# Weight tiles of the T-form matmuls placed by 64-byte residue: high parts at 64, low parts at 0 modulo 128

## The chip, the cores and the metric

The kernel runs on one core of one Trainium2 chip. The metric is the device time of one execution in microseconds; the number quoted is the median over runs. One further execution was profiled; its rows are what the prediction reads.

## What is computed

The reference is a block of two layers followed by a second block, for 256 tokens of width 1024, all in float32:

```python
for l in range(2):
    h = _rmsnorm(x, norm_mix[l])
    p_rw, p_sb, p_ret, p_conv = jnp.split(h @ w_in[l], MIX_SPLITS, axis=-1)
    branches = (_rwkv7_mixer(p_rw, ...), _stick_breaking_mixer(p_sb, ...),
                _retention_mixer(p_ret, ...), _conformer_conv_mixer(p_conv, ...))
    merged = sum(sigmoid(h @ w_gate[l, i]) * (branches[i] @ w_branch[l, i]) for i in range(4))
    x = x + merged @ w_out[l]
    h = _rmsnorm(x, norm_ffn[l])
    x = x + (_swiglu(h, ffn_w1, ffn_w3, ffn_w2) if l == 0 else _moe_ffn(h, router, moe_w1, moe_w3, moe_w2))
x = second_block(x, ...)     # attention and a recurrence on h @ w_in_2, then w_out_2
```

(The sum over branches is written shorter here than in the source.) What matters for this change is that nearly all of the time goes into products of activations with weight matrices that are read once from HBM. The feed-forward of layer 0 is 1024 by 2816; that of layer 1 is a mixture of eight experts.

## The kernel before, in words

**Split products.** A float32 product is made of three float32r matmuls. A weight block of 128 by 1024 floats (4096 bytes per partition) arrives in a `raw` tile; `wsplit_` (L258) makes a high part `wh` on ScalarE (L271) and a low part `wl = raw - wh` on VectorE (L272). The activations have been split the same way, into `hh` and `hl` (in other stages `uh`/`ul`, `bh`/`bl`, `mh`/`ml`, and so on). Each product is then `wh` with the high activations, `wh` with the low ones, and `wl` with the high ones, summed in one PSUM bank. All matmuls go through one wrapper and carry line L131 in the profile.

**Two forms.** In the T form the weights are the stationary operand, 128 by 128, and 256 tokens of an activation tile are streamed past them, so that every matmul has a weight load of its own:

```python
if kind == "T":
    ps = ((h[:, kk, off:off + n], ah), (h[:, kk, off:off + n], al), (o[:, kk, off:off + n], ah))
```

(`dense`, L332; `h` is `wh`, `o` is `wl`, `ah` and `al` are the activations; the feed-forward's second product, `down` at L1792, does the same.) In the other form the activations are stationary and up to 512 columns of the weights are streamed. The program has 5,904 T-form matmuls of 256 columns. The layers' input projections, gates, branch outputs, the feed-forward of layer 0, and most of the second block are T form; the experts and a few input columns are the other form.

**Slots.** `slot` (L242) hands out the tiles in turn. Pool `wp` has three slots for `raw` and three for each of `wh` and `wl`; a stage can add spare slots of its own pool with `spare` (L254). The feed-forward of layer 0 has two split slots of its own (`spare(fp, 4, 2)`, L1785): its split blocks go to three `wp` slots, then two of its own, and round again, 24 matmuls to each block. The mixture of experts has two of its own as well.

**Addresses.** The tiles lie in SBUF in the order in which they are first asked for. `pad` (L168) takes up bytes between them. The activations of the layers were padded to a start of 0 modulo 128 bytes. In the built program, starts modulo 128 bytes are:

| tile | before | with the change |
|---|---|---|
| `wp` slots, `wh` / `wl` | 64 / 64 | 64 / 0 |
| feed-forward's own slots, `wh` / `wl` | 0 / 0 | 64 / 0 |
| experts' own slots, `wh` / `wl` | 64 / 64 | 64 / 64 |
| `hh`, `hl`, `uh`, `ul`, `mh`, `ml`, `nr` | 0 | 0 |
| `bh`, `bl` of the branches, but for one | 0 | 0 |
| `bl` of branch 0 in layer 0 | 64 | 64 |
| `yah` in the second block | 96 | 96 |
| experts' activations `xg`, `mu` | 64 | 64 |

Columns inside a weight tile are taken in steps of 128 floats (512 bytes), rows of a tile in steps of 1024 or more bytes, so every operand has the residue of its tile.

The order of the work is set by a scheduler that takes priorities from the code (`tc.high_priority`) and a few dependencies written out by hand.

Of the kernel before, what the change touches and what calls it, by code (L numbers as in the profile page):

```python
# [18 lines left out]
P = 128  # L19
# [89 lines left out]
def build(tc, I, out, dbg=None, upto=99):  # L109
# [11 lines left out]
    wp = es.enter_context(tc.tile_pool(name="wp", bufs=4))  # L121
# [26 lines left out]
    def bank(tag="mx"):  # L148
        return pp.tile([P, 512], F32, name=tag, tag=tag, bufs=4)
# [18 lines left out]
    def pad(pool, n, nm):  # L168

        pool.tile([P, n // 4], F32, name=nm, tag=nm, bufs=1)  # L170
# [55 lines left out]
    def wsplit(raw, k, n, perm=False):  # L226

        with tc.high_priority(offset=HP[0]):
            return wsplit_(raw, k, n, perm)

    HP = [0, 0]


    more = {"pool": None, "raw": 0, "split": 0, "few": 0, "lead": 0}
    turn = {"raw": 0, "split": 0}


# [1 line left out]
    lead = {"n": 0, "ops": (), "hold": (), "late": None}  # L239
    behind = []  # L240

    def slot(kind, shapes):  # L242
        own = more[kind]
        n = 3 + own
        t_ = n - 1 if more["few"] else turn[kind] % n
        turn[kind] += 1
        at = min(more["lead"], own)

        if t_ < at or t_ >= at + 3:
            t_ -= 3 * (t_ >= at)  # L250
            return [more["pool"].tile(sh, dt, name=nm, tag=f"{nm}x{t_}", bufs=1) for nm, sh, dt in shapes]
        return [wp.tile(sh, dt, name=nm, tag=nm, bufs=3) for nm, sh, dt in shapes]

    def spare(pool, raw, split_, lead=0):  # L254
        more.update(pool=pool, raw=raw, split=split_, few=0, lead=lead)
        turn.update(raw=0, split=0)

    def wsplit_(raw, k, n, perm):  # L258
        h, o = slot("split", [("wh", [P, 1024], F32R), ("wl", [P, 1024], F32R)])
        h = h[:, :k * n].rearrange("p (k n) -> p k n", n=n)  # L260
        o = o[:, :k * n].rearrange("p (k n) -> p k n", n=n)
        if perm:
            for g in range(2):
                src = raw[:, :, g * 256:(g + 1) * 256].rearrange("p k (b d) -> p k b d", d=64)
                hv = h.rearrange("p k (b g d) -> p k g b d", g=2, d=64)[:, :, g]
                ov = o.rearrange("p k (b g d) -> p k g b d", g=2, d=64)[:, :, g]
                for kk in range(k):
                    S.copy(out=hv[:, kk], in_=src[:, kk])
                    V.tensor_sub(out=ov[:, kk], in0=src[:, kk], in1=hv[:, kk])
        else:  # L270
            a = S.copy(out=h, in_=raw)  # L271
            i = V.tensor_sub(out=o, in0=raw, in1=h)  # L272
            if lead["n"]:
                lead["n"] -= 1
                if lead["late"] and not lead["n"]:
                    tc.add_manual_dep(i.ins, lead["late"].ins.name, nosync, reason="choice first")
                for x, y in zip((a, i), lead["ops"]):
                    tc.add_manual_dep(x.ins, y.ins.name, nosync, reason="activations first")
                for r in lead["hold"]:
                    tc.add_manual_dep(r.ins, i.ins.name, nosync, reason="first half first")  # L280
                lead["hold"] = ()
            if behind:
                for x, y in zip((a, i), behind.pop(0)):
                    tc.add_manual_dep(x.ins, y.ins.name, nosync, reason="norm first")
        return h, o

    def wload(src, k, n, rows=False, pinned=False, halves=False):
        with tc.high_priority(offset=HP[1]):
            return wload_(src, k, n, rows, pinned, halves)
# [222 lines left out]
    def run(g):  # L512
        for _ in g:
            pass
# [10 lines left out]
    def mix_layer(l):  # L525
        with ExitStack() as ls_:
# [315 lines left out]
            def raised():  # L842
                HP[0], HP[1] = 500, 500
                yield
# [202 lines left out]
            for g in range(2):  # L1047
                _, gb = dense(I["w_gate"][l, 0], g * 512, 512, KC, hact, TJ)
                if g:
                    HP[0], HP[1] = 0, 0  # L1050
                for c in range(2):
# [329 lines left out]
    def second():  # L1381
        W = I["w_in_2"]
        with ExitStack() as ss_:
# [26 lines left out]
            next(lg)  # L1410
            HP[0], HP[1] = 500, 500
            run(lg)
# [362 lines left out]
    for l in range(2):  # L1775
        if upto < 2 * l + 1:
            break
        mix_layer(l)

        if upto < 2 * l + 2:  # L1780
            break
        if l == 0:
            with ExitStack() as fs:
                fp = fs.enter_context(tc.tile_pool(name="ffn", bufs=2, reuse_waits="tile"))
                spare(fp, 4, 2)  # L1785
                placed(None)
                hact = norm(gains("nf", l, 2), fp, "fth", 12, halves=True)
                accs = [bank() for _ in range(4)]
                first = {}
                F = 2816  # L1790

                def down(f0, uh, ul):  # L1792

                    for k0, ks, h, o in wstream(I["ffn_w2"][0][f0 * P:(f0 + 2) * P], 0, 1024, 2):
                        for kk in range(ks):
                            kc = f0 + k0 + kk
                            a0, a1 = uh[:, k0 + kk], ul[:, k0 + kk]
                            for b in range(KC):
                                acc = accs[b // 2][:, (b % 2) * T:(b % 2 + 1) * T]
                                cs = slice(b * P, (b + 1) * P)  # L1800
                                for q, (x_, m_) in enumerate(((h[:, kk, cs], a0), (h[:, kk, cs], a1), (o[:, kk, cs], a0))):
                                    st = kc == 0 and q == 0
                                    i = TE.matmul(acc, x_, m_, start=st and b % 2 == 0, stop=kc == F // P - 1 and q == 2, skip_group_check=True)
                                    if st and b % 2 == 0:
                                        first[b // 2] = i
                                    elif st:
                                        tc.add_manual_dep(i.ins, first[b // 2].ins.name, nosync, reason="bank order")

                ready = []
                for g0 in range(0, F, 512):  # L1810
                    cn = min(512, F - g0)
                    jobs = [("T", 128 * c, 128) for c in range(cn // P)]
                    _, ba = dense(I["ffn_w1"][0], g0, cn, KC, hact if g0 else late["early"], jobs)
                    if g0 == 0:
                        late["finish"]()
                    tts = []
                    for c in range(cn // T):
                        th = fp.tile([P, 512], F32, name="fth", tag="fth", bufs=12)
                        a_ = ba[2 * c]
                        if g0 == 0:  # L1820
                            a_ = fp.tile([P, 512], F32, name="fsc", tag="fth", bufs=12)
                            V.tensor_tensor(out=a_.rearrange("p (a b) -> p a b", b=T), in0=ba[2 * c].rearrange("p (a b) -> p a b", b=T), in1=late["rsb"], op=OP.mult)
                        S.activation(out=th, in_=a_, func=AF.Tanh, scale=0.5)
                        V.scalar_tensor_tensor(th, th, 1.0, a_, op0=OP.add, op1=OP.mult)
                        tts.append(th)
                    for r in ready:
                        down(*r)
                    ready = []
                    _, bb = dense(I["ffn_w3"][0], g0, cn, KC, hact, jobs)
                    for c in range(cn // T):  # L1830
                        th = tts[c]
                        V.tensor_tensor(out=th, in0=th, in1=bb[2 * c], op=OP.mult)
                        uh = fp.tile([P, 2, T], F32R, name="uh", tag="uh", bufs=4)
                        ul = fp.tile([P, 2, T], F32R, name="ul", tag="ul", bufs=4)
                        split(th.rearrange("p (a b) -> p a b", b=T), uh, ul)
                        ready.append((g0 // P + 2 * c, uh, ul))
                    if g0 == LL[0]:
                        lc = late_constants(fp, late_loads(fp))
                    if g0 >= LL[1]:
                        next(lc, None)  # L1840
                placed("ffn")
                run(lc)
                for r in ready:
                    down(*r)
                for q in range(4):
                    residual(accs[q], 2 * q)
                spare(None, 0, 0)
        else:
            moe(gains("nf", l, 2))
        dump(f"xf{l}", xT)  # L1850
# [37 lines left out]
```

## Time and profile before

| | |
|---|---|
| median of 3 runs | 1419.56 us (1419.38 to 1420.79) |
| profiled execution | 1418.68 us, its span 1416.9 us |
| TensorE (PE) busy | 1361.9 us, 96% of the span, 10,953 matmuls |
| weight loads (PEld) | 1262.1 us, 89%, 10,953 loads |
| VectorE (DVE) busy | 1078.2 us, 76% |
| ScalarE (ACT) busy | 805.4 us, 57% |
| mean granted TensorE clock | 0.992 |
| HBM | 292 MB moved, 206 GB/s over the span |

How to read it: the busy time of a matmul in the trace is the time from its start to the end of its last write, and neighbours overlap; a matmul that is reported with 282 ns can follow its predecessor after 113 ns. The time that a stretch of matmuls takes is therefore read from the starts in the timeline: last start minus first start, divided by the number of steps between them. Busy shares count overlapping work once.

### The profile page before, as it was taken

How to read it: one execution, taken by the hardware profiler on the slowest of the kernel's cores; microseconds unless marked ns; L12 is line 12 of the kernel's file. 1: busy time of each engine (PE TensorE's matmuls, PEld its weight loads, DVE VectorE, ACT ScalarE, POOL GpSimd, SP SyncE). 2: the span in 40 equal slices, each digit the busy share in tenths (PEclk: the TensorE clock that was granted, in tenths of full speed). 3: DMA queues.
4: the chain of work that ended last, by engine and by line, in shares of the span. 5: the costliest groups of instructions: out<-in, count | busy, mean ns of one | idle time of the engine just before them, and what ended most of it. 6: DMA issues, size and time to landing. Idle time of an engine off the chain costs nothing. (4 is left out here: it accounts for less than half of the span.)

```text
span 1416.9 us, 26493 instructions
## 1 busy us (share of the span) xinstructions
PE 1361.9 (96%) x10953; PEld 1262.1 (89%) x10953; DVE 1078.2 (76%) x1569; ACT 805.4 (57%) x1126; POOL 51.3 (4%) x65
## 2 busy tenths in 40 slices
PE   6999989999999899999998899999999999999998
PEld 6989979999999889988898788888888887998997
DVE  5669867685655585897576798998998999676765
ACT  5543264564444454324544688788788777465653
POOL 0000010001000100002000000000000002010000
PEclk9999999999999999999999899999999999999999
DMA  7553125586565345412457799899899896743352
GB/s 257 182 170 104 62 94 194 190 301 207 180 139 204 119 141 179 148 62 96 131 186 278 246 363 368 280 375 360 293 379 339 309 339 209 228 145 120 103 135 91
DMA packets 138098, 294.24 MB, mean 208 GB/s; under 512 B 6981, under 2 KB 29517, under 8 KB 137712
## 3 DMA queue, kind: packets, MB, share of 16 engines
q1 hardware_dynamic: 134720, 283.14, 58.0%
q0 software_dynamic: 3168, 9.31, 2.7%
q8 instruction: 87, 1.43, 0.4%
q14 instruction: 43, 0.35, 0.1%
q10 hardware_dynamic: 80, 0.02, 0.0%
HBM read 289.82 MB, written 2.62 MB: 206 GB/s over the span
## 5 line engine op out<-in xcount | busy, mean ns | idle before, releaser
L272 DVE TENSOR_TENSOR wl<-raw,wh 128x1024 fp32r<-128x1024 f32 (+1 forms) x542 | 633.5, 1187 | 220.8 <-ACT wh L271 215.1
L271 ACT CAST wh<-raw 128x1024 fp32r<-128x1024 f32 (+1 forms) x542 | 549.2, 1022 | 424.4 <-PE mm L131 336.0
L131 PE MATMUL mm<-hh,wl 128*128 128x256 f32 x1376 | 388.0, 282 | 5.6 <-DVE wl L272 3.1
L131 PE MATMUL mm<-hh,wh 128*128 128x256 f32 x1376 | 391.1, 284 | 2.3 <-ACT hh L223 1.6
L131 PE MATMUL mm<-hl,wh 128*128 128x256 f32 x1376 | 389.9, 283 | 0.2 <-DVE hl L224 0.2
L131 PEld LDWEIGHTS mm<-hh,wl 128*128 128x128 f32 x1376 | 260.7, 190 | 7.5 <-DVE wl L272 3.5
L131 PEld LDWEIGHTS mm<-hh,wh 128*128 128x128 f32 x1376 | 261.0, 190 | 6.7 <-issue 2.7
L131 PEld LDWEIGHTS mm<-hl,wh 128*128 128x128 f32 x1376 | 260.8, 190 | 3.4 <-issue 1.8
L131 PE MATMUL mm<-wh,xg 128*128 128x512 f32 (+1 forms) x768 | 229.4, 374 | 0.0
L131 PEld LDWEIGHTS mm<-wh,xg 128*128 128x128 f32 x768 | 142.6, 188 | 20.0
L131 PE MATMUL mm<-wl,xg 128*128 128x512 f32 (+1 forms) x384 | 142.6, 371 | 0.0
L131 PE MATMUL mx<-wh,mu 128*128 128x512 f32 x352 | 117.3, 394 | 0.0
L131 PEld LDWEIGHTS mm<-wl,xg 128*128 128x128 f32 x384 | 72.2, 188 | 9.9
L131 PEld LDWEIGHTS mx<-wh,mu 128*128 128x128 f32 x352 | 66.1, 188 | 12.7
L131 PE MATMUL mx<-wl,mu 128*128 128x512 f32 x176 | 68.8, 391 | 0.0
L975 DVE SCALAR_TENSOR_TENSOR cac<-cu,pcd,cac 128x256 f32<-128x256 f32 x120 | 52.8, 477 | 0.1
L131 PE MATMUL mx<-uh,wh 128*128 128x256 f32 x176 | 49.0, 281 | 1.4 <-ACT uh L223 1.4
L131 PE MATMUL mx<-ul,wh 128*128 128x256 f32 x176 | 49.4, 281 | 0.0
L131 PE MATMUL mx<-uh,wl 128*128 128x256 f32 x176 | 49.2, 280 | 0.0
L131 PE MATMUL mm<-nr,wh 128*128 128x256 f32 x192 | 36.8, 287 | 3.7 <-ACT nr L460 2.1
L131 PEld LDWEIGHTS mx<-wl,mu 128*128 128x128 f32 x176 | 33.1, 188 | 5.6
L131 PE MATMUL mm<-bh,wh 128*128 128x256 f32 x128 | 35.6, 281 | 0.2 <-DVE gth L1031 0.2
(686 smaller groups left out, 2065.2 us busy)
## 6 DMA issues: line engine op xcount, KB each, us to landing
raw<-in_moe_w_dram SPq DMA_DIRECT2D x104, 1024.0 KB
raw<-in_w_in_dram SPq DMA_DIRECT2D x42, 1024.0 KB
raw<-in_ffn_w_dram SPq DMA_DIRECT2D x33, 1024.0 KB
raw<-in_w_gate_dram SPq DMA_DIRECT2D x32, 1024.0 KB
raw<-in_moe_w_dram SPq DMA_DIRECT2D x32, 768.0 KB
raw<-in_w_out_dram SPq DMA_DIRECT2D x12, 1024.0 KB
raw<-in_w_branch_dram SPq DMA_DIRECT2D x8, 1024.0 KB
raw<-in_moe_w_dram SPq DMA_DIRECT2D x8, 512.0 KB
```

Of the source, the lines that this page charges most:

```text
L131: i = getattr(nc.tensor, name)(*a, **k)
L271: a = S.copy(out=h, in_=raw)
L272: i = V.tensor_sub(out=o, in0=raw, in1=h)
L975: V.scalar_tensor_tensor(acc[:, b], cu[:, b, 2 + k:2 + k + T], dw[:, 2 * k + b:2 * k + b + 1], acc[:, b], op0=OP.mult, op1=OP.add)
```

## The change

The change moves tiles and nothing else. A new helper `tile_` allocates the split tiles: in `wp` it puts a pad of 64 bytes ahead of the first `wl` tile and one of 448 behind the last; in a stage that asks for it (`shift=1`, the feed-forward of layer 0) it pads 64 bytes ahead of the first own `wh` tile, makes the own `wh` and `wl` tiles 1040 floats wide, of which the same 1024 are used, and pads 192 bytes behind the last. The pads add up so that all other tiles move by 512 or 1024 bytes and keep their residues modulo 512. The instructions of every engine and queue, and their order, are the same as before; only addresses differ.

```diff
--- before.py
+++ after.py
@@ -228,10 +228,12 @@
         with tc.high_priority(offset=HP[0]):
             return wsplit_(raw, k, n, perm)
 
+
+    SHIFT = (64, 448), (0, 0), (64, 192)
     HP = [0, 0]
 
 
-    more = {"pool": None, "raw": 0, "split": 0, "few": 0, "lead": 0}
+    more = {"pool": None, "raw": 0, "split": 0, "few": 0, "lead": 0, "shift": 0}
     turn = {"raw": 0, "split": 0}
 
 
@@ -248,11 +250,26 @@
 
         if t_ < at or t_ >= at + 3:
             t_ -= 3 * (t_ >= at)
-            return [more["pool"].tile(sh, dt, name=nm, tag=f"{nm}x{t_}", bufs=1) for nm, sh, dt in shapes]
-        return [wp.tile(sh, dt, name=nm, tag=nm, bufs=3) for nm, sh, dt in shapes]
-
-    def spare(pool, raw, split_, lead=0):
-        more.update(pool=pool, raw=raw, split=split_, few=0, lead=lead)
+            return [tile_(more["pool"], sh, dt, nm, f"{nm}x{t_}", 1) for nm, sh, dt in shapes]
+        return [tile_(wp, sh, dt, nm, nm, 3) for nm, sh, dt in shapes]
+
+    seen = set()
+
+    def tile_(pool, sh, dt, nm, tag, bufs):
+
+        new, own = (id(pool), tag) not in seen, pool is not wp
+        seen.add((id(pool), tag))
+        lo, hi = SHIFT[1 + more["shift"] if own else 0]
+        if new and tag == ("whx0" if own else "wl") and lo:
+            pad(pool, lo, "padw")
+        wide = {(False, "wl"): 1024}.get((own, nm), 1040 if own and more["shift"] else sh[1])
+        t = pool.tile([P, wide], dt, name=nm, tag=tag, bufs=bufs) if nm != "raw" else pool.tile(sh, dt, name=nm, tag=tag, bufs=bufs)
+        if new and tag == (f"wlx{more['split'] - 1}" if own else "wl") and hi:
+            pad(pool, hi, "padz")
+        return t
+
+    def spare(pool, raw, split_, lead=0, shift=0):
+        more.update(pool=pool, raw=raw, split=split_, few=0, lead=lead, shift=shift)
         turn.update(raw=0, split=0)
 
     def wsplit_(raw, k, n, perm):
@@ -1782,7 +1799,7 @@
         if l == 0:
             with ExitStack() as fs:
                 fp = fs.enter_context(tc.tile_pool(name="ffn", bufs=2, reuse_waits="tile"))
-                spare(fp, 4, 2)
+                spare(fp, 4, 2, shift=1)
                 placed(None)
                 hact = norm(gains("nf", l, 2), fp, "fth", 12, halves=True)
                 accs = [bank() for _ in range(4)]
```

## Rows read from the trace of the kernel before

**Rows 1.** Page: busy time and chain of waits (chain shares of the span by engine).

```profile
PE 1361.9 (96%) x10953; PEld 1262.1 (89%) x10953; DVE 1078.2 (76%) x1569; ACT 805.4 (57%) x1126; POOL 51.3 (4%) x65
PE 41%; DVE 2%; ACT 1%; issue 0%; POOL 0%; DVEq 0%; ACTq 0%
```

**Rows 2.** Windows: stretch (us), its length, PE busy (instructions), clock, DMA share, GB/s.

```profile
225.00:300.00 75.00, 74.79 (x639) 1.00 0.66 222
300.00:480.00 180.00, 176.45 (x1481) 1.00 0.59 182
...
785.00:1190.00 405.00, 404.88 (x2045) 0.99 0.92 329
```

**Rows 3.** Groups of matmuls by form: busy us, mean ns; 128x256 is the T form.

```profile
L131 PE MATMUL mm<-hh,wh 128*128 128x256 f32 x1376 | 391.1, 284 | 2.3 <-ACT hh L223 1.6 <-DVE pcv L213 0.4 <-ACT wh L271 0.3
...
L131 PE MATMUL mm<-wl,xg 128*128 128x512 f32 x256 | 99.8, 390 | 0.0
L131 PE MATMUL mx<-wl,mu 128*128 128x512 f32 x176 | 68.8, 391 | 0.0
```

**Rows 4.** Timeline, PE: start us, duration us; first and last start, feed-forward, `wp` slots.

```profile
325.08 0.28 PE L131 MATMUL mm<-hl,wh 128*128 128x256 f32 x1
...
330.52 0.28 PE L131 MATMUL mx<-ul,wh 128*128 128x256 f32 x1
```

**Rows 5.** Timeline, PE, feed-forward, the own slots that follow.

```profile
330.87 0.28 PE L131 MATMUL mx<-ul,wh 128*128 128x256 f32 x1
...
336.27 0.28 PE L131 MATMUL mx<-ul,wh 128*128 128x256 f32 x1
```

**Rows 6.** Timeline, PE, feed-forward later: `wp` slots, first and last start.

```profile
350.66 0.28 PE L131 MATMUL mm<-hl,wh 128*128 128x256 f32 x1
...
358.79 0.28 PE L131 MATMUL mm<-hl,wh 128*128 128x256 f32 x1
```

**Rows 7.** Timeline, PE, feed-forward later: own slots.

```profile
359.02 0.28 PE L131 MATMUL mm<-hh,wh 128*128 128x256 f32 x1
...
364.42 0.28 PE L131 MATMUL mx<-uh,wh 128*128 128x256 f32 x1
```

**Rows 8.** Timeline, PE, layer 0: branch outputs 3, 1 and 2, first and last.

```profile
223.29 0.28 PE L131 MATMUL mm<-bh,wh 128*128 128x256 f32 x1
...
238.93 0.28 PE L131 MATMUL mm<-bh,wh 128*128 128x256 f32 x1
```

**Rows 9.** Timeline, PE, layer 0: branch output 0, two stretches without a pause.

```profile
240.92 0.28 PE L131 MATMUL mm<-bh,wl 128*128 128x256 f32 x1
...
242.10 0.28 PE L131 MATMUL mm<-bh,wl 128*128 128x256 f32 x1
...
242.68 0.28 PE L131 MATMUL mm<-bh,wl 128*128 128x256 f32 x1
...
245.16 0.28 PE L131 MATMUL mm<-bh,wl 128*128 128x256 f32 x1
```

**Rows 10.** Timeline, PE, layer 0: the last gate, first and last start.

```profile
245.28 0.28 PE L131 MATMUL mm<-hh,wh 128*128 128x256 f32 x1
...
267.53 0.28 PE L131 MATMUL mm<-hh,wh 128*128 128x256 f32 x1
```

**Rows 11.** Timeline, PE: 512 weight columns past `hh`/`hl`, then past `xg` in the experts.

```profile
72.59 0.39 PE L131 MATMUL mm<-wh,hh 128*128 128x512 f32 x1
...
83.55 0.39 PE L131 MATMUL mm<-wh,hl 128*128 128x512 f32 x1
...
799.93 0.39 PE L131 MATMUL mm<-wl,xg 128*128 128x512 f32 x1
...
802.65 0.39 PE L131 MATMUL mm<-wl,xg 128*128 128x512 f32 x1
```

**Rows 12.** Instructions on tile `wl`, VectorE, 301 to 476 us: ns min/median/max.

```profile
L272 DVE TENSOR_TENSOR wl<-raw,wh x62: 1217/1225/1227, 300.4 to 475.1; 128x1024 fp32r<-128x1024 f32 x62
```

## The prediction, before the run

> **What bounds the kernel.** I read the page first. TensorE is busy for 96% of the span and its weight loads for 89%, so a load runs beside the matmul ahead of it; the chain of waits that ended last names hardly anything but PE [rows 1]. The chain stops early, so I checked it by stage with the windows view: in the gates and branch outputs of layer 0 PE is busy for 74.79 of 75.00 us, in the feed-forward for 176.45 of 180, in the experts for 404.88 of 405, with the clock granted in full or nearly [rows 2]. What changes the step from one matmul to the next therefore reaches the end of the kernel almost undiminished. The table of matmul forms says where the matmuls are: 1,376 each of the three products with `hh`/`hl`, and smaller groups, 5,904 in T form in all [rows 3]. Its mean of 284 ns is no price, since neighbours overlap. Prices come from the timeline, as last start minus first start over the steps between.
>
> **What an address costs, as the trace of before shows it.** The feed-forward holds the comparison ready-made: its blocks go to three `wp` slots (weights at 64, activations at 0 modulo 128; I call that *opposite*), then to two own slots (both at 0, *equal*). Stage, engines and clock are the same. Opposite: 325.08 to 330.52 is 48 steps in 5.44 us, 113.3 ns each [rows 4]. Equal: 330.87 to 336.27 is 45 steps in 5.40 us, 120.0 ns [rows 5]. So residues matter by 6.7 ns a matmul. But opposite is not always that fast: later in the same stage 69 steps take 8.13 us, 117.8 ns [rows 6], while the own slots still take 45 steps in 5.40 us, 120.0 ns [rows 7]. The fast pace also holds in branch outputs 3, 1 and 2, 138 steps in 15.64 us, 113.3 ns [rows 8]. It comes and goes with the same addresses, mostly after a pause or a change of operand. I call the two a *fast* and a *slow* pace of opposite operands. The stage of mostly T-form work gives the mean over both: 75.00 us over 639 matmuls, 117.4 ns [rows 2].
>
> **The change part by part.** No instruction is added, removed or moved on any engine or DMA queue; there is no new wait. Only the spacing of matmuls, and of the engines that read or write the moved tiles, can change.
>
> *VectorE and ScalarE* write the tiles at other residues. In the feed-forward the low parts of `wp` and own slots, at 64 and at 0, take 1217 to 1227 ns, median 1225 [rows 12]. I cost this at nothing, and by the spread of that row a difference of 10 ns on 542 splits could be 5 us of VectorE time at most, in stages where it has slack beside PE.
>
> *T-form matmuls.* A triple now has two loads at 64 and one at 0, all against activations at 0. By neighbouring pairs that is opposite, opposite, equal. Layer 0 holds one stage with such a triple: branch output 0, where it is the low activations that lie at 64 beside weights at 64, so that of three pairs one is equal. There 10 steps take 1.18 us and 21 steps 2.48 us, 3.66 us over 31, 118.1 ns [rows 9]. It follows directly on the fast stretch [rows 8] and does not keep its pace. The slow pace of the gate right behind it, 189 steps in 22.25 us, is 117.7 ns [rows 10]. I take 118.1 ns for every T-form matmul, since this is the only row with the new mixture, against a mean of 117.4: 5,904 x 0.7 ns = **+4.1 us**. In this mean the feed-forward's 26 own blocks gain (26 x 24 x 1.9 ns = 1.2 us), and the rest loses, above all where it was fast. The bounds: if the fast pace holds and only the equal pair pays, (2 x 113.3 + 120.0)/3 = 115.5 ns, 5,904 x -1.9 = -11 us; if the slow one does, (2 x 117.8 + 120.0)/3 = 118.5, +6.5 us. Outside those lie fast everywhere, 113.3, -24 us, and 120.0 everywhere, +15 us.
>
> *The experts* stream weights past `xg` and `mu`, all at 64 so far, 12 steps in 2.72 us, 226.7 ns for 512 columns. With residues apart, as past `hh`/`hl`, 47 steps take 10.96 us, 233.2 ns [rows 11]. Here it is equal that is cheaper. Of the 256 + 176 low products of that width [rows 3], three in five lie in `wp` slots and now stand apart: 259 x 6.5 = **+1.7 us**, at least nothing, and at most 2.2 us if 77 narrower ones pay too. The 64 low products of 512 columns past activations at 0 go the other way: **-0.4 us**.
>
> The sum is +4.1 + 1.7 - 0.4 = +5.4 us. On the profiled execution, 1418.68 us, that is 1424.1; the median of the runs shown stands 0.88 us above it, so the forecast for the median is **1424.9 us**. A measurement of this kernel tells about 0.2% (2.8 us) from no change.
>
> **A rule against the rows.** The rows 4 and 5 show weights read from two residues at 113.3 and 120.0 ns with all else alike. The Trainium skill, page "SBUF — State Buffer", section "SBUF: two separate sides", states that TensorE has ports of its own and never waits on another reader, and the section on bandwidth pools gives its weight loads a second, independent read port. By that rule no address would matter and the sum would be 0, 1419.6 us; the trace disagrees by 6.7 ns a matmul.
>
> **The rivals.**
>
> *Faster, the slow pace is broken.* If the slow pace is a lock between two streams of constant distance, a load that is displaced by 64 bytes once in three may keep it from forming, and the triple costs two fast steps and an equal one, 115.5 ns: 1419.6 - 11 + 1 = about 1410 us. The new rows would decide it by whether 117.8 is seen at all. For it: the fast pace exists with the very same addresses. Against it: the mixed stage left the fast pace at once [rows 8, 9], and the own slots, equal for 48 matmuls on end, did not break the slow one [rows 6, 7]. I give it 0.22, and 0.10 more to something faster still or to gains by halves (113.3 ns everywhere would be 1395 us).
>
> *No change that can be measured.* The gain of the own blocks (1.2 to 2.8 us, the latter if they come to 115.5), a part of the fast stretches kept, and experts that pay nothing, together cancel the loss; or residues act otherwise than by pairs, and paces are drawn anew with a mean near 117.4. That gives 1417 to 1422 us. 0.20, of which a few hundredths stand for residues that do not matter at all, as if what I read as their price were the own slots' place.
>
> *Worse than forecast.* The equal load drags the whole triple to 120.0 ns, as when all three are equal [rows 5, 7]: 5,904 x 2.6 = +15 us, 1435 us. 0.04.
>
> *The forecast*, triples near 118 ns: 0.44.
>
> **How the numbers follow.** The forecast and the worse case give slower 0.48; no change 0.20; faster 0.32. The range goes from the broken lock, 1409 us (1419.6 - 11, experts free), to the slow pace with its equal load and the experts at full price, 1419.6 + 6.5 + 2.2 = 1428.3 us. It leaves out the all-fast case and the 120 ns case. The forecast's own range is 1421.5 to 1428.3 us.
>
> **What would show it.** Right: in the profile of the changed kernel the steps in the gates and input projections stand near 118 ns, no long stretch at 113.3 is left, the feed-forward's own blocks come down from 120.0, and low products of the experts in `wp` slots step at over 230 ns. Wrong: long stretches at 115.5 or less, which would mean that the mixed stage of layer 0 misled me because there it was the streamed operand that jumped by 64 bytes and not the loaded one; or experts at 227 ns throughout, which takes 1.7 us off.

## The result, and the profile after

The changed kernel takes **1426.91 us** (median of 6 runs, 1424.53 to 1428.93) against 1419.62 us (6 runs) for the kernel before on the same chip: ratio 1.0052, 95% interval 1.0038 to 1.0065. It is slower by 7.3 us. The forecast was 1424.9 us, within a range to 1428.3.

The profiled execution of the changed kernel was the slowest of its six, 1428.93 us with a span of 1427.2 us; that of the kernel before was, with 1418.68 us, quicker than all of its runs. Part of the 10.3 us between the two spans is therefore the draw of two executions, and the text keeps that part apart.

The page of the changed kernel, busy times and chain:

```profile
PE 1372.8 (96%) x10953; PEld 1268.9 (89%) x10953; DVE 1079.0 (76%) x1569; ACT 805.0 (56%) x1126; POOL 51.4 (4%) x65
PE 40%; DVE 2%; ACT 1%; issue 1%; POOL 0%; ACTq 0%; DVEq 0%
```

Beside [rows 1], PE's busy time has grown by 10.9 us with the same 10,953 matmuls, and its weight loads by 6.8; VectorE and ScalarE stand within 1 us of where they were. The low tiles take as long to write as in [rows 12], here on VectorE from 305 to 482 us (min/median/max in ns):

```profile
L289 DVE TENSOR_TENSOR wl<-raw,wh x61: 1217/1225/1228, 305.3 to 479.3; 128x1024 fp32r<-128x1024 f32 x61
```

The same three stretches as in [rows 2], each moved by as much as the stage now starts later (length, then PE, weight loads, VectorE, ScalarE and GpSimd busy, then clock, DMA share, GB/s):

```profile
227.70:302.70 75.00, 75.00 (x638) 74.77 (x637) 59.13 (x77) 40.91 (x52) 0.52 (x1) 1.00 0.64 221
304.70:484.70 180.00, 176.44 (x1469) 174.66 (x1469) 106.29 (x137) 78.13 (x90) 8.21 (x15) 0.99 0.58 179
791.80:1196.80 405.00, 404.63 (x2030) 348.52 (x2031) 373.18 (x398) 317.20 (x372) 1.02 (x2) 1.00 0.92 329
```

PE has no new gap in these stages; it gets through fewer matmuls in the same time: 2,030 for 2,045 in the experts, 1,469 for 1,481 in the feed-forward. The two differ in kind. In the feed-forward the clock of 0.99 holds one stretch of 3.4 us at half the clock, which by itself costs some 14 steps (an estimate: half of 3.4 us over 118 ns); outside it the mean T-form step there is 117.9 ns against 118.0. In the experts the steps themselves are longer. The groups by form say which kinds (busy us, mean ns), first of the changed kernel:

```profile
L131 PE MATMUL mm<-hl,wh 128*128 128x256 f32 x1376 | 391.9, 285 | 0.2 <-DVE hl L224 0.2
L131 PE MATMUL mm<-hh,wh 128*128 128x256 f32 x1376 | 391.8, 285 | 2.3 <-ACT hh L223 1.6 <-DVE pcv L213 0.4 <-ACT wh L288 0.3
L131 PE MATMUL mm<-wh,xg 128*128 128x512 f32 x512 | 163.7, 394 | 0.0
L131 PE MATMUL mx<-wh,mu 128*128 128x512 f32 x352 | 118.2, 397 | 0.0
L131 PE MATMUL mm<-wl,xg 128*128 128x512 f32 x256 | 100.6, 393 | 0.0
L131 PE MATMUL mx<-wl,mu 128*128 128x512 f32 x176 | 69.2, 393 | 0.0
```

Then the experts' high products in the kernel before, which the prediction had not looked at:

```profile
L131 PE MATMUL mm<-wh,xg 128*128 128x512 f32 x512 | 162.2, 391 | 0.0
...
L131 PE MATMUL mx<-wh,mu 128*128 128x512 f32 x352 | 117.3, 394 | 0.0
```

The low products went up as forecast, from 99.8 to 100.6 and from 68.8 to 69.2 [rows 3]; but so did the high ones, by 1.5 and 0.9 us, although their tiles had not moved.

The timeline of the changed kernel, first and last start of the stretches that [rows 4], [rows 5], [rows 8] and [rows 11] hold (start us, duration us):

```profile
329.79 0.28 PE L131 MATMUL mm<-hl,wh 128*128 128x256 f32 x1
...
335.44 0.28 PE L131 MATMUL mx<-ul,wh 128*128 128x256 f32 x1
...
335.79 0.28 PE L131 MATMUL mx<-ul,wh 128*128 128x256 f32 x1
...
341.11 0.28 PE L131 MATMUL mx<-ul,wh 128*128 128x256 f32 x1
...
226.02 0.28 PE L131 MATMUL mm<-bh,wh 128*128 128x256 f32 x1
...
242.33 0.28 PE L131 MATMUL mm<-bh,wh 128*128 128x256 f32 x1
...
75.11 0.40 PE L131 MATMUL mm<-wh,hh 128*128 128x512 f32 x1
...
86.13 0.39 PE L131 MATMUL mm<-wh,hl 128*128 128x512 f32 x1
...
806.75 0.40 PE L131 MATMUL mm<-wl,xg 128*128 128x512 f32 x1
...
809.50 0.39 PE L131 MATMUL mm<-wl,xg 128*128 128x512 f32 x1
```

| stretch | steps | before, ns | after, ns |
|---|---|---|---|
| feed-forward, `wp` slots | 48 | 113.3 | 5.65 / 48 = 117.7 |
| feed-forward, own slots | 45 | 120.0 | 5.32 / 45 = 118.2 |
| branch outputs 3, 1, 2 | 138 | 113.3 | 16.31 / 138 = 118.2 |
| 512 columns past `hh`, `hl` | 47 | 233.2 | 11.02 / 47 = 234.5 |
| 512 columns past `xg` | 12 | 226.7 | 2.75 / 12 = 229.2 |

The last row of the table needs care: seven of its twelve steps lie in a block from the experts' own slots, where no tile moved. The block ahead of it, from `wp` slots with the low tile displaced, takes 17 steps in 3.95 us, about 232 ns; the one from the own slots takes 11 steps in 2.52 us, about 229 ns. Before, both stood at about 227 ns:

```profile
801.64 0.39 PE L131 MATMUL mm<-wh,xg 128*128 128x512 f32 x1
...
805.59 0.40 PE L131 MATMUL mm<-wh,xg 128*128 128x512 f32 x1
...
805.83 0.39 PE L131 MATMUL mm<-wh,xg 128*128 128x512 f32 x1
...
808.35 0.39 PE L131 MATMUL mm<-wh,xg 128*128 128x512 f32 x1
```

**Where the 10.3 us are.** Both traces hold the same matmuls in the same order, so each step (from a start to the next) can be set against its counterpart. The columns give the mean step; "past `xg`" means that weights are streamed past `xg` as the stationary operand. Of steps without a pause in either trace:

| kind | steps | before, ns | after, ns | difference |
|---|---|---|---|---|
| T form | 5,555 | 117.39 | 117.78 | +2.1 us |
| 512 columns past `xg` | 758 | 227.20 | 230.58 | +2.6 us |
| 512 columns past `mu` | 513 | 228.77 | 231.43 | +1.4 us |
| 512 past `hh`, `mh`, `hl`, `ml`; 256 past `hh` | 254 | 204.7 | 206.4 | +0.4 us |
| steps with the clock at half in either | 190 | 205.3 | 231.0 | +4.9 us |
| all others | 3,682 | | | about -1 us |

The +4.9 us is the draw. It is PE at 1.2 instead of 2.4 GHz in stretches that lie elsewhere from one execution to the next, 25.5 us of them in the first trace and 37.1 in the second. Behind the feed-forward this execution shows such a stretch, and a second execution of the same kernel (run e12, below) shows none in the same window; last but two in the row is the granted clock:

```profile
488.00:500.00 12.00, 9.51 (x56) 9.10 (x55) 9.18 (x20) 7.39 (x14) 0.96 (x2) 0.72 0.38 131
```

```profile
488.00:500.00 12.00, 10.16 (x84) 9.96 (x85) 10.32 (x24) 8.39 (x17) 0.71 (x1) 1.00 0.50 166
```

Over the runs the mean granted clock of the two kernels is the same, 0.9888 (the 48 runs of before that stood beside e1 to e8) and 0.9887 (6 of the change), so nothing on record gives it a part in the 7.3 us between the medians. The other rows come near them: 2.1 + 2.6 + 1.4 + 0.4 = 6.5 us, and 7.7 us in a second pair of traces (e11 and e12, below), with the interval of the ratio from 5.4 to 9.2 us.

### The profile page after: what moved, and what is told of

Same layout as the page of the kernel before. It is cut to its first block, busy times and chain, and to the rows that moved or that the text cites. A ratio compares the mean times of both kernels' runs of the same rounds, so it can differ in the third digit from the quotient of the medians.

```text
span 1427.2 us, 26495 instructions
## 1 busy us (share of the span) xinstructions
PE 1372.8 (96%) x10953; PEld 1268.9 (89%) x10953; DVE 1079.0 (76%) x1569; ACT 805.0 (56%) x1126; POOL 51.4 (4%) x65
## 5 line engine op out<-in xcount | busy, mean ns | idle before, releaser
L131 PE MATMUL mx<-wh,mu 128*128 128x512 f32 x352 | 118.2, 397 | 0.0
L131 PE MATMUL mx<-wl,mu 128*128 128x512 f32 x176 | 69.2, 393 | 0.0
L131 PE MATMUL mm<-nr,wh 128*128 128x256 f32 x192 | 40.4, 306 | 3.7 <-ACT nr L477 2.1
L131 PEld LDWEIGHTS mm<-nr,wh 128*128 128x128 f32 x192 | 32.7, 207 | 4.5 <-ACT nr L477 2.5
```

What stands on the lines that cost most here:

```text
L131: i = getattr(nc.tensor, name)(*a, **k)
```

## The experiments

Each of the kernels computes all of the reference. Ratios are to the kernel before on the same chip. "Distance" is the address of the weights less that of the activations, modulo 256 bytes: for the T form before it was 192 with `wp` slots and 0 with the feed-forward's own, against activations at 0 modulo 256, which most of them are. The branch outputs of layer 0 have theirs at 128, so that [rows 8] stand at the distance 64, not 192. "T mean" is the mean T-form step without a pause, at the full clock.

### The change in halves

**e1: only `wp`.** The feed-forward's own slots stay at 0 and 0.

```diff
-                spare(fp, 4, 2, shift=1)
+                spare(fp, 4, 2)
```

> Low parts of the wp slots at 0, the feed-forward's own slots left at 0/0 as before. Theory P (the price hangs on the residues of neighbouring operands, pair by pair): T-form steps outside the own slots at 117.8 ns with no stretch at 113.3, own slots at 120.0, experts' 512-column steps near 230.5 ns; slower than before by about as much as the change, plus some 1 us for the own slots (624 x 2 ns): 1426 to 1429 us. Rival C (the loss is mostly time at the half clock, drawn afresh for each execution or program, and residues shift little): the steps move by under 1 ns, the time lies anywhere between 1419 and 1428 us and goes with the granted clock.

1428.63 us, ratio 1.0067 [1.0054, 1.0080]; T mean 117.98 ns, and the stretch of the own slots again 45 steps in 5.40 us, 120.0 ns. So moving the own slots is the part of the change that gains, some 1 to 2 us by the steps; the intervals of the two ratios, 1.0052 and 1.0067, overlap.

**e2: only the own slots.**

```diff
-    SHIFT = (64, 448), (0, 0), (64, 192)
+    SHIFT = (0, 0), (0, 0), (64, 192)
```

> Only the feed-forward's own split slots at 64/0; wp slots left at 64/64. Theory P: the own slots come from 120.0 to 117.8 ns or a little less, 624 x 2.2 = 1.4 us gained, all else as before (fast stretches at 113.3 in the first layer kept): 1418 us, at most 2.8 us gained. Rival C: no step change that shows, 1417 to 1426 us with the clock.

1418.80 us, ratio 0.9998 [0.9986, 1.0010]: no change that can be told. The own slots step as in the full change, 45 steps in 5.32 us:

```profile
332.29 0.28 PE L131 MATMUL mx<-ul,wh 128*128 128x256 f32 x1
...
337.61 0.28 PE L131 MATMUL mx<-ul,wh 128*128 128x256 f32 x1
```

**e3: the T form as the change has it, the experts as before; e4: the reverse.** The `wl` tiles of `wp` are 64 floats wider and start 16 floats further on in one of the two kinds of stage. The lines of e3 (in e4 the 0 and the 16 are swapped and the own slots stay):

```diff
-    SHIFT = (64, 448), (0, 0), (64, 192)
+    SHIFT = (0, 256), (0, 0), (64, 192)
+    LOW = {"off": 16}
...
-        wide = {(False, "wl"): 1024}.get((own, nm), 1040 if own and more["shift"] else sh[1])
+        wide = {(False, "wl"): 1088}.get((own, nm), 1040 if own and more["shift"] else sh[1])
...
-        return t
+        return t[:, LOW["off"]:LOW["off"] + 1024] if nm == "wl" and not own else t
...
             spare(fp, *own, 3)
+            LOW["off"] = 0
...
             spare(None, 0, 0)
+            LOW["off"] = 16
```

> The change in all T-form stages, but the experts read their low parts from wp slots at 64 as before (same tiles, another start inside them). Theory P: experts' 512-column steps back at 227 to 228 ns, which takes back the 3.9 us that the experts' steps cost in the profile of the change; T-form steps stay at 117.8: about 1423 us at the clock of the change, 1421 to 1424. Rival C: as slow as the change, 1425 to 1428 us, since the T-form stages and their clock set it.

> The other half: T-form stages as before (64/64, own slots 0/0), the experts' low parts in wp slots at 0. Theory P: experts' 512-column steps at 230 to 231 ns, all three products of a triple and not the low one alone; T-form mean 117.4 with stretches at 113.3: 3.9 us slower than before, 1423 to 1424 us. Rival C: 1419 to 1420 us at the clock of before, whatever the steps do.

e3: 1422.44 us, ratio 1.0030 [1.0019, 1.0042]. e4: 1422.58 us, ratio 1.0031 [1.0019, 1.0043]. Either half costs about 3 us and the two together, 1.0061, agree with the whole within its interval. The groups by form of e3, then of e4:

```profile
L131 PE MATMUL mm<-wh,xg 128*128 128x512 f32 x512 | 162.2, 391 | 0.0
...
L131 PE MATMUL mm<-wl,xg 128*128 128x512 f32 x256 | 99.8, 390 | 0.0
```

```profile
L131 PE MATMUL mm<-wh,xg 128*128 128x512 f32 x512 | 163.7, 394 | 0.0
...
L131 PE MATMUL mm<-wl,xg 128*128 128x512 f32 x256 | 100.6, 393 | 0.0
```

In e3 the experts' steps are those of the kernel before to 0.01 ns (227.20 and 228.77), in e4 those of the change to 0.1 ns (230.50 and 231.42). The residue of the low tile alone makes the high products slower too. In e4 the T form, left as before, has a mean of 117.0 ns instead of the 117.4 that were expected, a first sign that the fast pace is not taken alike in every trace.

### Which residue it is

**e5: every T-form weight at the distance 192 from activations at 0,** the own slots included.

```diff
-    SHIFT = (64, 448), (0, 0), (64, 192)
+    SHIFT = (0, 0), (0, 0), (192, 320)
...
-        wide = {(False, "wl"): 1024}.get((own, nm), 1040 if own and more["shift"] else sh[1])
+        wide = {(False, "wl"): 1024}.get((own, nm), sh[1])
```

> The other way to mend the feed-forward's own slots: high and low parts both at 64, like the wp slots, which stay at 64/64; activations at 0. Theory P (pairs): no equal pair is left in a T-form stage, so the own slots step at one of the two opposite paces, 117.8 or 113.3 ns, and no T-form stretch at 120.0 is left; 624 x 2.2 to 6.7 ns = 1.4 to 4.2 us gained on before, 1415.5 to 1418.5 us. Rival M (the mixture 64/0 is itself what brought the own slots to 117.8, uniform placement at 64 does not help): own slots stay near 120, 1419 to 1420 us.

1420.44 us, ratio 1.0004 [0.9993, 1.0015]: a miss. No step class at 120.0 is left, and these slots step at 117.8 ns, yet only 5% of the T steps took 112 to 115 ns (called fast below), against 15% in the first trace of before, and the mean was 117.58. One trace does not tell whether that is the edit or the draw. The fast pace does appear, where the first trace of before had it too (95 steps from 29.2 us), 95 steps in 10.77 us, 113.4 ns:

```profile
29.05 0.28 PE L131 MATMUL mm<-hl,wh 128*128 128x256 f32 x1
...
39.82 0.28 PE L131 MATMUL mm<-hh,wh 128*128 128x256 f32 x1
```

**e7: weights as before, but the low activations `hl` at 64 modulo 128.** Here the streamed operand alternates and the loaded one does not.

```diff
-        hh, hl = ap_.tile([P, KC, T], F32R, name="hh", tag="acth", bufs=1), ap_.tile([P, KC, T], F32R, name="hl", tag="actl", bufs=1)
-        pad(ap_, 448, "padb")
+        hh = ap_.tile([P, KC, T], F32R, name="hh", tag="acth", bufs=1)
+        pad(ap_, 192, "padc")
+        hl = ap_.tile([P, KC, T], F32R, name="hl", tag="actl", bufs=1)
+        pad(ap_, 256, "padb")
```

> The mirror of the change: weights stay at 64/64, the low activations hl of the layers move to 64 (192 modulo 256), hh stays at 0. One of three pairs is equal again, this time through the streamed operand. Theory P: stages that stream hh and hl step at 117.5 to 118.5 ns with no stretch at 113.3 in them, as in the changed kernel; the feed-forward's second product (uh, ul still at 0) and own slots as before. 1421 to 1424 us. Rival L (only a displaced load matters, not the distance between load and stream): hh/hl stages as before, fast stretches kept, 1419 to 1420 us.

1422.67 us, ratio 1.0024 [1.0012, 1.0037]; T mean 118.33 ns. The gate of [rows 10] takes 189 steps in 22.48 us, 118.9 ns, and no stage with `hh` and `hl` shows the fast pace:

```profile
248.75 0.28 PE L131 MATMUL mm<-hh,wh 128*128 128x256 f32 x1
...
271.23 0.28 PE L131 MATMUL mm<-hh,wh 128*128 128x256 f32 x1
```

So the fast pace is lost whichever of the two operands is moved, but the price is not the same: 118.9 ns here, 117.8 in the change. One thing the distance does not explain: the branch outputs of layer 0, none of whose operands moved, step at 117.8 ns here (138 steps in 16.25 us) and at 113.3 in [rows 8].

**e8: high parts at 0, low parts at 64,** in `wp` and in the own slots, so that two of three pairs are equal.

```diff
-    SHIFT = (64, 448), (0, 0), (64, 192)
+    SHIFT = (64, 0), (0, 0), (0, 256)
...
-        if new and tag == ("whx0" if own else "wl") and lo:
+        if new and tag == ("whx0" if own else "wh") and lo:
             pad(pool, lo, "padw")
+        if new and tag == "wl" and not own:
+            pad(pool, 448, "padv")
```

> The change with the parts exchanged: high parts at 0, low parts at 64, in wp and own slots; two of three pairs are equal. Theory P by addition: T-form (117.8 + 2 x 120.0)/3 = 119.3 ns, 5,904 x 1.9 = 11 us over before, and the experts' steps at 230 ns or more (4 us or over): about 1435 us. Rival S (any mixture settles near 117.8, however many pairs are equal): T-form 117.8, 1424 to 1428 us.

1428.18 us, ratio 1.0059 [1.0041, 1.0078]. The T mean is 117.73 ns, not nearer to 120.0 than in the change: with weights at two residues the mean over the T form is 117.75 whether one or two of three pairs are equal, as the rival expected. Single steps alternate in such a mixture (17 to 24% of them fall between 112 and 115 ns without any stretch at 113.3), so the share of fast steps is a measure only for kernels with one residue.

### The other side

**e6: all T-form weights 64 bytes ahead of the activations instead of 64 behind,** distance 64 in place of 192; modulo 128 these are the same.

```diff
-    SHIFT = (64, 448), (0, 0), (64, 192)
+    SHIFT = (128, 384), (0, 0), (64, 448)
...
-        if new and tag == ("whx0" if own else "wl") and lo:
+        if new and tag == ("whx0" if own else "wh") and lo:
...
-        wide = {(False, "wl"): 1024}.get((own, nm), 1040 if own and more["shift"] else sh[1])
+        wide = {(False, "wl"): 1024}.get((own, nm), sh[1])
```

> All split weights of the T-form stages (wp and own slots, high and low) at 64 modulo 256 instead of 192; activations at 0. Theory P as stated, with residues modulo 128 alone: the same two opposite paces as before in a like mixture, mean 117 to 117.4 ns, 1416 to 1420 us. Rival Q (the fast pace hangs on the distance modulo 256, since in layer 0 it held where activations at 128 ran against weights at 192): the pace is 113.3 ns wherever activations lie at 0 modulo 256, some 4,500 x 4.4 ns = 20 us gained, 1400 us, and 117.8 in layer 0's branch outputs instead.

1417.85 us, ratio 0.9983 [0.9972, 0.9995]. T steps have a mean of 115.27 ns, 58% of them at 112 to 115: 11.8 us gained on the first trace of before. The rival was right that 64 and 192 differ, but not that every stage would be fast. The experts gave back 4.3 us, since their `wp` weights now stand at a distance of 128 from `xg` and `mu` (230.90 and 231.62 ns over all their blocks). In the blocks from `wp` slots alone it is 233.0 ns past `xg`, as in these 17 steps of 3.97 us:

```profile
791.63 0.40 PE L131 MATMUL mm<-wh,xg 128*128 128x512 f32 x1
...
795.60 0.39 PE L131 MATMUL mm<-wh,xg 128*128 128x512 f32 x1
```

Steps gain 7.5 us in this sum, the medians only 2.3 us (1420.17 - 1417.85); e9 shows the same shortfall.

**e9: the same, with the experts' weights back at the distance 0,** and **e10: the same again, with the stages whose activations lie at 128 modulo 256 at the distance 64 too** (branch outputs 1 to 3 of layer 0, branch output 0 of layer 1, and the output projection of both layers; the steps that stream activations at 0 in those stages, `bh` of branch 0 in layer 0 and half of `ml`, come to 192 by it). The `wp` tiles are 32 floats wider and start in one of two places:

```diff
-    SHIFT = (64, 448), (0, 0), (64, 192)
+    SHIFT = (0, 256), (0, 0), (64, 448)
+    LOW = {"at": 64, "wh": 0, "wl": 0}
...
-        wide = {(False, "wl"): 1024}.get((own, nm), 1040 if own and more["shift"] else sh[1])
+        wide = 1056 if not own and nm != "raw" else sh[1]
+        if not own and nm != "raw":
+            n = LOW[nm]
+            LOW[nm] += 1
+            start = (192, 64)[((n + (n > 467)) % 3 == 2) ^ (nm == "wl")]
+            off = 0 if start == LOW["at"] else 32
+            return t[:, off:off + 1024]
...
             spare(fp, *own, 3)
+            LOW["at"] = 192
...
             spare(None, 0, 0)
+            LOW["at"] = 64
```

In e10 further lines of the same kind set `LOW["at"]` ahead of those stages and back behind them.

> The weights of the T-form stages stay where the run 'other side' had them (64 modulo 256, ahead of activations at 0), and the experts read theirs at 192 modulo 256 as before the change, equal to xg and mu: the tiles are 32 words wider and start in one of two places. Theory A (the pace of a matmul depends on the distance of the two addresses modulo 256, in both forms, and nothing else is different): the T form keeps its mean of 115.3 ns (fast pace in half of the steps or more), the experts' 512-column steps come back from 230.9 and 231.6 to 227.2 and 228.8 ns, which is 4.3 us less than the other side's 1417.9: about 1413.5 us, ratio 0.9957. Rival B (the share of the fast pace is drawn anew with every program, and the other side's 58% was a good draw): T mean anywhere from 116.8 to 117.6 ns, so 1418 to 1421 us, ratio 0.999 to 1.001. Rival C (the experts' price lies not in residues modulo 256 but in the slots having been moved at all): their steps stay at 230.9, about 1418 us.

> As the run before it, and the stages of layer 0 and 1 whose activations lie at 128 modulo 256 (branch outputs, branch output 0, and the output projection's low activations) read weights at 192 instead of 64, so that they too stand 64 modulo 256 ahead of what is streamed. Theory A (distance 64 modulo 256 is what lets the fast pace form): the branch outputs and mixed stages, 117.8 ns in the other-side run where their distance was 192, come to 113.3 ns in half of the steps or more; some 500 matmuls by 2 to 4.5 ns are 1 to 2 us: 1412 us, ratio 0.995, 0.999 of the run before. Rival B: those stages show either pace as before, no measurable difference from the run before, and the other stages' shares differ between the two programs as much as these do.

e9: **1413.93 us, ratio 0.9954 [0.9941, 0.9968]**, and e10: 1414.50 us, ratio 0.9962 [0.9949, 0.9976]. Theory A held for e9 in each number: T mean 115.26 ns, experts 227.20 and 228.77 as before the change. The timeline of e9: 742 steps of the feed-forward in 84.09 us, 113.3 ns (in the kernel before 118.7); the gate of [rows 10], 189 steps in 21.45 us, 113.5; and 12 steps past `xg` in 2.72 us, 226.7:

```profile
385.70 0.28 PE L131 MATMUL mm<-hh,wh 128*128 128x256 f32 x1
...
469.79 0.28 PE L131 MATMUL mm<-hl,wh 128*128 128x256 f32 x1
...
245.86 0.28 PE L131 MATMUL mm<-hh,wh 128*128 128x256 f32 x1
...
267.31 0.28 PE L131 MATMUL mm<-hh,wh 128*128 128x256 f32 x1
...
797.30 0.39 PE L131 MATMUL mm<-wl,xg 128*128 128x512 f32 x1
...
800.02 0.39 PE L131 MATMUL mm<-wl,xg 128*128 128x512 f32 x1
...
73.06 0.39 PE L131 MATMUL mm<-wh,hh 128*128 128x512 f32 x1
...
83.82 0.39 PE L131 MATMUL mm<-wh,hl 128*128 128x512 f32 x1
```

The last two are 512 columns past `hh` and `hl`: 47 steps in 10.76 us, 228.9 ns (233.2 before).

Not all of the gain arrives. T steps give some 12 us between the first trace of before and that of e9; the medians differ by 6.4 (1420.29 - 1413.93). In that pair of traces the steps with the clock at half took back 8.8 us, and the mean granted clock over the five runs is 0.987 against 0.988 in the nine of before beside them; for e6 it is 0.988 against 0.989, for e10 0.986 against 0.988. Whether shorter steps bring more time at half the clock was not tested.

e10 is a miss: it does not differ from e9. The branch outputs of layer 0, now at the distance 64, kept the slow pace, 138 steps in 16.26 us, 117.8 ns:

```profile
223.25 0.28 PE L131 MATMUL mm<-bh,wh 128*128 128x256 f32 x1
...
239.51 0.28 PE L131 MATMUL mm<-bh,wh 128*128 128x256 f32 x1
```

The distance 64 lets the fast pace form far more often, but does not compel it.

### Both kernels profiled again

**e11: the kernel before; e12: the changed kernel,** neither with any edit.

> The kernel before, unchanged, profiled a second time: is its share of fast T-form steps (15% between 112 and 115 ns in the first profile) a property of its addresses or drawn in each execution? Theory A (drawn): the stretches at 113.3 ns lie elsewhere this time, while the steps that are not drawn are the same to 0.1 ns: own feed-forward slots 120.0, experts 227.2 and 228.8. The T mean lies between 116.9 and 117.6, which is up to 4 us of the span between two executions of one kernel. Rival B (fixed by the addresses and the order): the same stretches at 113.3, as at 325 us and at 223 us, T mean 117.4.

> The changed kernel, unchanged, profiled a second time. Theory A (its mixture has only one pace): T mean 117.8 within 0.1 and no stretch at 113.3 ns; experts 230.6 and 231.4; what differs from its first profile, whose span was 1427.2 us, lies in the stretches at half clock. Rival B: a stretch at 113.3 ns appears, so that the mixture too has a fast pace which the first profile merely did not draw.

e11 took 1419.19 us, e12 1424.44 us, one run each. Theory A held for e12. For e11 it held in part: the steps that it called not drawn and the T mean came as it said, and some fast stretches moved, but the two that rival B had named were fast again. Two stretches of the kernel before, first in its first trace, then in e11:

```profile
20.65 0.28 PE L131 MATMUL mm<-hh,wh 128*128 128x256 f32 x1
...
28.13 0.28 PE L131 MATMUL mm<-hh,wl 128*128 128x256 f32 x1
...
385.98 0.28 PE L131 MATMUL mm<-hh,wh 128*128 128x256 f32 x1
...
474.06 0.28 PE L131 MATMUL mm<-hl,wh 128*128 128x256 f32 x1
```

```profile
21.26 0.28 PE L131 MATMUL mm<-hh,wh 128*128 128x256 f32 x1
...
29.04 0.28 PE L131 MATMUL mm<-hh,wl 128*128 128x256 f32 x1
...
389.13 0.28 PE L131 MATMUL mm<-hh,wh 128*128 128x256 f32 x1
...
475.23 0.28 PE L131 MATMUL mm<-hl,wh 128*128 128x256 f32 x1
```

The first 66 steps went from 113.3 to 117.9 ns (7.48 and 7.78 us), the 742 steps of the feed-forward from 118.7 to 116.0 (88.08 and 86.10 us): with the same program and addresses, fast stretches lie elsewhere. The stretches of [rows 4] and [rows 8] were fast again, and all the fast stretches of e11 (means of 12 steps) are fast in the trace of e4 too, whose T form has the same distances; so not all is redrawn. The share of fast T steps was 15% and 20%, the mean 117.39 and 117.14 ns. The changed kernel had 117.77 and 117.75 and in neither trace a stretch at 113.3. Between e11 and e12 the T steps differ by 3.4 us, those past `xg` and `mu` by 2.5 and 1.4, and the steps with the clock at half this time by -1.3.

## Why the prediction was right

**The direction and the cause held.** No engine, queue or wait changed; the steps of PE did, and what they lost reached the end: 6.5 and 7.7 us in the two pairs of traces, 7.3 between the medians. (What steps gain did not all reach it, as e6 and e9 show.) The Trainium skill, page "SBUF — State Buffer", section "SBUF: two separate sides", states that TensorE has ports of its own and never waits on others. Read as the prediction read it, for TensorE's own two streams, it would have given no change, and that misses 7.3 us here and 6.4 us the other way in e9, with addresses as the only difference. Whether it holds against the reads of other engines no run here shows.

**T form: forecast +4.1 us, measured +2.1 and +3.4** in the two pairs of traces. The step "118.1 ns for every T-form matmul" took the mixture from 31 steps; over 5,500 it is 117.75 to 117.78. The base of 117.4 was one draw; a second gave 117.1. The two errors partly cancel. That 118.1 came so near is in part luck: in [rows 9] it is the streamed operand that alternates, and e7, which does that in all the stages with `hh` and `hl`, stands at 118.8 ns in them, not at 117.8. The prediction also counted residues modulo 128 and took [rows 4] and [rows 8] for the same addresses; modulo 256 they stand at 192 and at 64, and e6 shows that these two differ. That the own blocks gain held (120.0 to 118.2), and so did the sign that was to show it: no long stretch at 113.3 was left.

**Experts: forecast +1.7 us with an upper bound of 2.2, measured +3.9** (+2.6 and +1.4). This is the step that failed: "259 x 6.5" charged the low products of 512 columns alone, as if a high product beside a displaced low one were not touched. Its sign, over 230 ns in `wp` slots, came true, but for all three products. The groups show the high products up by 2.4 us and the low by 1.2, and e4 shows it with nothing of the T form changed. The rows past `hh` were no price for it: there every operand stands at one distance, here two alternate. In blocks from `wp` slots the steps past `xg` rose by 5.2 ns (227.0 to 232.2) instead of 6.5, high and low products alike, and in blocks from the own slots, where nothing moved, still by 1.8 (227.0 to 228.8).

**Low products past activations at 0: forecast -0.4 us, measured +0.4.** The same error: steps past `hl` fell by 3 ns, but those past `hh` rose by as much, and there are twice as many.

**The sum.** With 2.1 to 3.4, 3.9 and 0.4 it is 6.4 to 7.7 us; the medians differ by 7.3. The forecast of 5.4 came so near by luck in its terms: a T term somewhat too large stood beside an expert term of less than half the measured size.

**The rivals.** "No change" fell by the interval of the ratio, 1.0038 to 1.0065. "The slow pace is broken" fell: displaced loads ended the fast pace and left the slow one, as [rows 9] had suggested of the mixture. The nearest to it is the output projection, half of whose steps now meet three distances (64, 128 and 192): four stretches of 47 steps at 115.9 ns in both traces, but each was at 117.6 to 117.9 before. "Worse than forecast" fell as well: an equal load does not drag its triple to 120.0, and two of three do not either (e8). The prediction's pairs, which would price a triple as the mean of its three, are no model: by them e8 would have gone to 119.3.

**Left open.** What makes a stretch take the fast or the slow pace is not known; it is drawn at least in part. Why two addresses matter to each other at all is not shown either: the runs show the distance and the step, not what lies between. The distance 128 occurs in the T form only within mixtures (for instance, in the change, between `wl` and the branch outputs of layer 0, 118.2 ns). Of other distances, `yah` had 224 before and 96 in e9, beside `yal` at 192 and 64, with 117.8 ns in both; none was tried on purpose.

## What to carry to other kernels

Where PE is the bound and every matmul has its own weight load, the start addresses of loaded and streamed tiles modulo 256 bytes can be a tuning knob. In this kernel the placements tried lie between 0.995 and 1.007 of the time before. Read the step between starts in the timeline, and move a whole set of tiles that are used in turn: moving one part of it cost time in e1, e4, e7 and e8. A tile shared by stages of different forms has to suit both, and an offset inside a wider tile does that without moving anything else. A pace that is drawn needs more than one profile before a mean is taken as the base of a forecast.

## What was not expected of the hardware

- The distance has to be taken modulo 256, not 128: 64 and 192 differ, and so do 0 and 128. T form by distance (weights less activations): 0 gives 120.0 ns a step, 192 gives 113.3 or 117.8 with 5 to 24% fast (five traces), 64 gives the same two with 58 to 60% fast (three kernels). In the other form, 512 columns, by the same distance: `xg` at 0, 227.2; at 128, 233.0; `hh` at 192, 233.3; at 64, 228.9.
- Tiles that alternate between two residues change the pace of all that is used in turn with them: 117.75 ns on average in the T form whether one or two of three pairs are equal (from 115.9 to 118.2 by stage in the change); past `xg` all three members of a triple went from 227 to 232, the two that had not moved as well.
- The same program on the same addresses can take 113.3 or 117.8 ns in the same stretch from one execution to the next.
- e9 had the lowest median although its profile had most of the half clock, 45.8 us in all against 25.5 in the first trace of before.
